# Second layer: latent queries and one gate block with 512 moving columns over two weight places

## The chip, the cores and the metric

One core of a Trainium2 chip runs the whole forward pass. The metric is the device time of one execution in microseconds (us). The kernel before was timed three times; the median is 1577.26 us (1575.3 to 1577.57).

## What is computed

A backbone of two layers over 1024 latent tokens and 256 context tokens, all with 1024 features. Layer 1 is windowed attention with 16 heads. Layer 2 is latent attention, which the change concerns:

```
hx = rms_norm(x) * (1 + scale) + shift               # 1024 latent tokens; hc likewise, 256 context tokens
cq, ckv, kr, g = split(h @ w_in, [512, 256, 32, 1024])
q  = (rms_norm(cq, q_norm) @ w_uq)                   # 16 heads of 64 (nope) + 32 (rope)
kv = (rms_norm(ckv, kv_norm) @ w_ukv)                # 16 heads of 64 (keys) + 64 (values)
o  = softmax(q k^T) v                                # latent queries, context and latent keys
x  = x + gate * ((o * silu(g)) @ w_out)
```

A final RMSNorm gives the output. All inputs are float32. Of the second layer the change touches the product that gives `cq` (the latent queries, 512 columns) and a quarter of the product that gives `g` (the gates, 1024 columns).

## The kernel before, in words

Every product is split for precision: both operands are kept as a high and a low part, and `mm3` (L126 to L130) issues three matmuls for each block of 128 contracted features: high times high (L128), low times high (L129), high times low (L130). A matmul takes a stationary operand of 128 columns, loaded ahead of it, and streams the moving operand's columns; a PSUM bank of the kernel (`PB`) holds 512 of them.

The second layer's input is kept transposed in SBUF, in pairs of two token tiles: `hT1[p]` holds 256 tokens, pair 0 the context and pairs 1 to 4 the latent tokens. Each is 16 KB of a partition, in rows of 256 elements: eight rows (one for each 128 features) of the high part, then eight of the low part. The places, in KB of an arena: pair 0 at 134, pair 1 at 80, pair 2 at 0, pair 3 at 16, pair 4 at 32 (L981). The weights are loaded in ten blocks by `fetch1` (L1007): DMAs on SP into a ring of three stage buffers, then a split in two, the high part by ACT (L123), the low part by POOL or DVE (L124). A weight block of 256 columns has the same layout of 16 KB, and its place is given by `wst1` (L982): 96, 48, 96, 96, 48, 96, 64, 48, 96, 48. Blocks 1 and 2 are the two halves of the latent queries' weights (48 and 96), block 3 the rope queries' (96), blocks 4 and 5 the other queries' (48 and 96), blocks 6 to 9 the gates' (block 7 at 48, block 8 at 96, block 9 at 48).

The stages follow one another on TensorE (PE) in this order:

- keys and values (`kv_tile`) with gate block 6 between, from about 720 to 783 us;
- eight latent-query tiles (`cq_tile`, L1072), one for each 128 tokens: the tokens are the stationary operand, the weights the moving one, first the 256 columns of block 1, then those of block 2, eight rows and three matmuls each, 48 matmuls into the halves of one PSUM bank. Behind each: the sum of squares (ACT L1014), the root (POOL L1016), the scaling (DVE L1085); two tiles later four transposes (PE L1090) and a split by ACT and DVE into `cqT`, the transposed queries (high part at 64 to 80 KB of the same arena, low part in another arena);
- eight rope-query tiles (`qr_tile`, L1096), then sixteen tiles of the other queries (`qn_tile`), all with 512 moving columns, 12 matmuls each;
- gate block 7 for pairs 1 to 4 (`g_tile`, L1135, called at L1195): here the weights are stationary and a pair's 256 tokens the moving operand, 48 matmuls for each pair; ACT applies Silu to the 128x512 result (L1152) and SP stores it (L1154). Beside it the value and key weights are loaded and split (the value weights go to 64 to 80 KB, where the queries' high part was);
- block 9 is fetched behind block 7 into the same place (L1197); gate blocks 8 and 9 follow, partly within the attention;
- the attention, from about 949 us, in an order of PE, ACT and DVE that is written out by hand, and the output product between and behind.

Ahead of the attention the order of each engine's work is set by the Tile scheduler when the kernel is built, by program order as priority and by its own estimate of times. Waits between engines are set from what each instruction reads and writes.

Of the kernel before, what the change touches and what calls it, by code (L numbers as in the profile page):

```python
# [12 lines left out]
AF = mybir.ActivationFunctionType  # L13
# [10 lines left out]
NP = TOK // 256  # L24
EPS = 1e-6
KB = 256
# [21 lines left out]
def shp(ap, *dims):  # L48
    n = 1
    for d in dims:  # L50
        n *= d
    ap = ap[:, 0:n]
    if len(dims) == 1:
        return ap
    names = "abcdefg"[: len(dims)]
    kw = {c: d for c, d in zip(names[1:], dims[1:])}
    return ap.rearrange("p (" + " ".join(names) + ") -> p " + " ".join(names), **kw)
# [3 lines left out]
def kernel(ctx: ExitStack, tc: tile.TileContext, t, out, dbg=None):  # L61
    nc = tc.nc
# [5 lines left out]
    R = cpool.tile([128, int(R_KB * KB)], F32R, name="arena_r")  # L68
# [10 lines left out]
    g1_d = dpool.tile([8, 128, SEQ], F32, name="g1_d")  # L79
# [3 lines left out]
    load = nc.sync.dma_start  # L83
    load2 = nc.scalar.dma_start

    def r_at(kb, *dims):
        n = int(np.prod(dims))
        if kb >= 114:
            return shp(R2[:, int((kb - 114) * KB) : int((kb - 114) * KB) + n], *dims)
        return shp(R[:, int(kb * KB) : int(kb * KB) + n], *dims)  # L90
# [27 lines left out]
    pss = Banks(0, 1, 2, 3, 4, 5)  # L118
    pst = Banks(6, 7)

    def split(hi, lo, src, lo_eng=None):

        nc.scalar.copy(hi, src)  # L123
        (lo_eng or nc.vector).tensor_sub(lo, src, hi.bitcast(F32))  # L124

    def mm3(o, a, b, first, last):  # L126
        (ah, al), (bh, bl) = a, b
        nc.tensor.matmul(o, ah, bh, start=first, stop=False)  # L128
        nc.tensor.matmul(o, al, bh, start=False, stop=False)  # L129
        nc.tensor.matmul(o, ah, bl, start=False, stop=last)  # L130
# [174 lines left out]
    ev = Ring(F, [38, 40, 42, 44], 512)  # L305
# [17 lines left out]
    class Pieces:  # L323
# [6 lines left out]
        def load(self, n=1):  # L330
            for _ in range(n):
                if self.todo:
                    bi, k = self.todo.pop(0)
                    c0 = blocks[bi]
                    st = shp(stg.next(), 2, 256)
                    src = w_in[k * 128 : (k + 2) * 128, c0 : c0 + 256]
                    load(out=st, in_=src.rearrange("(k p) n -> p k n", p=128))
                    self.held.append((bi, k, st))
# [139 lines left out]
    def proj_t(bi, gp, c):  # L478

        W = wt[bi]  # L480
        ps = pss()
        if gp:
            o = shp(ps, 2, 256)
            m = [hw[gp][:, :, s] for s in range(2)]
        else:
            o = ps[:, 0:258]
            m = [hT[0][:, s] for s in range(2)]
        cs = slice(c * 128, c * 128 + 128)
        for k in range(8):
            b = [x[:, :, k, :] if gp else x[:, k, :] for x in m]  # L490
            mm3(o, [W[:, s, k, cs] for s in range(2)], b, k == 0, k == 7)
        if gp == 0:
            bias[bi, c] = biases()
            nc.scalar.copy(bias[bi, c], ps[:, 256:258])
        return ps
# [264 lines left out]
    class RawRing:  # L760
        i = 5
# [108 lines left out]
    for c in range(2):  # L870
        ps = proj_t(1, 0, c)
# [14 lines left out]
    for bi in (8, 9):  # L886
        for c in range(2):
            ps = proj_t(bi, 0, c)
# [40 lines left out]
    for ui, u in enumerate(units):  # L929
# [11 lines left out]
        for ci in range(u.m):  # L941
# [10 lines left out]
            i = u.g * u.m + ci - 1  # L952
# [28 lines left out]
    hT1 = [r_at(o, 2, 8, 256) for o in (134, 80, 0, 16, 32)]  # L981
# [11 lines left out]
    ev = Ring(F, [2, 4, 6, 12], 512)  # L993
# [8 lines left out]
    blocks1 = [("kv", 512, 288), ("cq", 0, 256), ("cq", 256, 256)]  # L1002
    blocks1 += [("qr", 1024, 512), ("qn", 0, 512), ("qn", 512, 512)]
    blocks1 += [("g", 800 + c * 256, 256) for c in range(4)]
    wt1 = {}

    def fetch1(bi, eng=None):  # L1007
        kind, c0, n = blocks1[bi]
        nk = 4 if kind[0] == "q" else 8
        wt1[bi] = r_at(wst1[bi], 2, nk, n)  # L1010
        load_w(wt1[bi], t["b_w_uq"] if kind[0] == "q" else w_in1, stg, nk, n, lo_eng=eng, col0=c0)

    def rstd(ps, n, st):
        nc.scalar.activation(junk[:, 0:n], ps, AF.Square, accum_out=st[:, 0:1])  # L1014
        nc.vector.tensor_scalar(st[:, 1:2], st[:, 0:1], 1.0 / n, EPS, ALU.mult, ALU.add)
        nc.gpsimd.tensor_tensor(st[:, 2:3], st[:, 1:2], mhalf, ALU.pow)  # L1016
        return st[:, 2:3]
# [22 lines left out]
    def kv_tile(ti):  # L1040
# [28 lines left out]

        pend.append(rest)  # L1070

    def cq_tile(ti):  # L1072
        p, j = (ti + 2) // 2, ti % 2
        ps = pss()
        for c in range(2):
            for k in range(8):
                mm3(
                    ps[:, c * 256 : c * 256 + 256],
                    [hT1[p][:, s, k, j * 128 : j * 128 + 128] for s in range(2)],
                    [wt1[1 + c][:, s, k, :] for s in range(2)],  # L1080
                    k == 0, k == 7,
                )
        r = rstd(ps, 512, sm_ring())
        e = ev.next()
        nc.vector.scalar_tensor_tensor(e, ps, r, qn, ALU.mult, ALU.mult)  # L1085

        def rest():
            pt = shp(pst(), 4, 128)
            for c in range(4):
                nc.tensor.transpose(pt[:, c, :], e[:, c * 128 : c * 128 + 128], ident)  # L1090
            ts = slice(ti * 128, ti * 128 + 128)
            split(cqT[0][:, :, ts], cqT[1][:, :, ts], pt)

        pend.append(rest)
# [40 lines left out]
    def g_tile(bi, p, half=None, bank=None):  # L1135
        c0 = blocks1[bi][1]
        W = wt1[bi]
        if half != 1:
            gps[bi] = pss() if bank is None else bank
        ps = gps[bi]  # L1140
        for j in (0, 1) if half is None else (half,):
            for k in range(8):
                mm3(
                    ps[:, j * 256 : j * 256 + 256],
                    [W[:, s, k, j * 128 : j * 128 + 128] for s in range(2)],
                    [hT1[p][:, s, k, :] for s in range(2)],
                    k == 0, k == 7,
                )
        if half == 0:
            return  # L1150
        gg = ev.next()
        nc.scalar.activation(gg, ps, AF.Silu)  # L1152
        ch = (c0 - 800) // 128
        load(out=g1_d[ch : ch + 2, :, (p - 1) * 256 : p * 256].rearrange("c p n -> p c n"), in_=shp(gg, 2, 256))  # L1154

    nx = norm_x(src1(4), xr, junk)
    for ti in range(NT):
        n = ti + 3
# [13 lines left out]
    for ti in range(8):  # L1172
        cq_tile(ti)
        flush(2)
# [13 lines left out]
    for k in range(2):  # L1188
        for c in range(4):
# [2 lines left out]
            dst = ukK if c < 2 else ukV  # L1192
            cs = slice((c % 2) * 512, (c % 2) * 512 + 512)
            split(dst[:, 0, k, cs], dst[:, 1, k, cs], st, nc.gpsimd)
    for p in range(1, NP):  # L1195
        g_tile(7, p)
    fetch1(9)  # L1197


# [532 lines left out]
```

## Time and profile before

| | |
|---|---|
| median of three runs | 1577.26 us |
| the profiled execution, device time | 1574.73 us |
| its span, first to last instruction | 1573.0 us |
| PE busy | 1538.7 us (98%), 9846 matmuls |
| PE's weight loads busy | 1228.6 us (78%) |
| VectorE (DVE), ScalarE (ACT), GpSimd (POOL) busy | 993.5, 772.8, 753.8 us |
| mean granted TensorE clock | 0.995 |

The profile shows one execution. Engines run side by side, so busy times do not add up to the span. "PE" are the matmuls, "PEld" their weight loads, which overlap the matmuls; SPq is the queue from which SP issues DMAs. Matmuls are pipelined: each lasts longer than the distance to the next one's start, and it is the distance that adds up. Rows of the order of time show the start, the duration, the engine, the line, the operation, what it writes and reads, the shape, a count where equal neighbours are merged, and in brackets the idle time ahead of it with what ended it.

### The profile page before, as it was taken

The page shows a single profiled execution, that of the slowest core. Times are in us where ns is not written, and L with a number is a line of the kernel's source. Part 1 is how long each engine was busy: PE and PEld are TensorE (multiplying, and loading weights), DVE is VectorE, ACT ScalarE, POOL GpSimd, SP SyncE. Part 2 cuts the span into 40 slices and gives each one's busy share as a digit, 9 for nine tenths or more (in the row PEclk, how much of TensorE's full clock was granted, in tenths as well). Part 3 has the DMA queues.
Part 4 walks back from the last instruction along what each step waited for, and adds up shares of the span by engine and source line. Part 5 has one row for each costly group of instructions (what it writes and reads, how often), then busy time and mean ns, then how long its engine had stood idle before and what let it go on. Part 6 is the DMA issues. An engine that isn't in the chain of part 4 may idle for free.

```text
span 1573.0 us, 26868 instructions
## 1 busy us (share of the span) xinstructions
PE 1538.7 (98%) x9846; PEld 1228.6 (78%) x9846; DVE 993.5 (63%) x1757; ACT 772.8 (49%) x1492; POOL 753.8 (48%) x810
## 2 busy tenths in 40 slices
PE   7999999999999999998999999999999999999998
PEld 4988888887878888888998899666766766766687
DVE  3878996657777777768425203666567566567354
ACT  4432322267777777767313323455555555555322
POOL 1151211136564444544105140588688688689410
PEclk9999999999999999999999999999999999999999
DMA  8357774653343222345105753313233233244251
GB/s 316 114 159 219 199 207 137 200 164 99 99 146 100 85 89 85 95 132 182 48 1 156 262 151 98 91 45 98 61 98 101 71 91 88 61 138 113 69 168 68
DMA packets 148277, 192.83 MB, mean 123 GB/s; under 512 B 13985, under 2 KB 86177, under 8 KB 148145
## 3 DMA queue, kind: packets, MB, share of 16 engines
q1 hardware_dynamic: 146672, 188.94, 40.2%
q10 hardware_dynamic: 1472, 2.16, 0.5%
q8 instruction: 78, 1.28, 0.3%
q14 instruction: 55, 0.44, 0.1%
HBM read 144.90 MB, written 46.15 MB: 121 GB/s over the span
## 4 chain that ended last, share of the span: by engine, by line
PE 81%; DVE 8%; issue 3%; DMA 3%; ACT 2%; POOL 2%; SPq 0%; DVEq 0%; POOLq 0%; ACTq 0%
PE PB L128 12%; PE PB L129 12%; PE PB L130 12%; PE PB L1359 12%; PE PB L1381 9%; PE PB L621 5%; PE PB L662 5%; PE PB L1322 4%; PE PB L652 4%; DVE arena_f L193 2%; DVE arena_f L519 1%; DMA arena_f<-a_w_in 1%; PE PB L1330 1%; PE PB L1410 1%; ACT arena_r L123 1%
## 5 line engine op out<-in xcount | busy, mean ns | idle before, releaser
L128 PE MATMUL PB<-arena_r 128*128 128x512 f32 (+3 forms) x1216 | 410.8, 339 | 5.5 <-ACT arena_r L423 2.4
L129 PE MATMUL PB<-arena_r 128*128 128x512 f32 (+3 forms) x1184 | 395.2, 334 | 1.8 <-POOL arena_r L689 0.8
L130 PE MATMUL PB<-arena_r 128*128 128x256 f32 (+3 forms) x1152 | 381.5, 332 | 0.2 <-DVE arena_r L124 0.2
L1373 POOL TENSOR_TENSOR arena_f<-arena_f 128x512 f32<-128x512 f32 x252 | 324.9, 1289 | 79.7 <-ACT arena_f L1365 62.9
L128 PEld LDWEIGHTS PB<-arena_r 128*128 128x128 f32 x1216 | 231.1, 191 | 32.2 <-ACT arena_r L423 4.8
L129 PEld LDWEIGHTS PB<-arena_r 128*128 128x128 f32 x1184 | 226.4, 191 | 22.9 <-DVE arena_r L424 2.4
L124 POOL TENSOR_TENSOR arena_r<-arena_f,arena_r 128x512 fp32r<-128x512 f32 x80 | 109.3, 1381 | 276.8 <-ACT arena_r L123 226.8
L130 PEld LDWEIGHTS PB<-arena_r 128*128 128x128 f32 x1152 | 220.4, 191 | 20.7 <-issue 1.7
L1365 ACT ACTIVATE arena_f<-PB 128x1024 f32<-128x1024 f32 x160 | 164.1, 1027 | 108.5 <-PE PB L1359 68.4
L1324 DVE TENSOR_REDUCE arena_f<-PB 128x1 f32<-128x1024 f32 x128 | 156.0, 1219 | 86.7 <-PE PB L1322 86.6
L1359 PE MATMUL PB<-arena_r 64*128 64x512 f32 (+1 forms) x1500 | 195.1, 392 | 0.3 <-ACT arena_f L1365 0.3
L1359 PEld LDWEIGHTS PB<-arena_r 64*128 64x128 f32 (+1 forms) x1500 | 137.1, 185 | 28.9 <-ACT arena_f L1365 1.8
L124 DVE TENSOR_TENSOR arena_r<-PB,arena_r 128x512 fp32r<-128x512 f32 x168 | 114.6, 689 | 61.1 <-ACT arena_r L123 60.2
L1381 PE MATMUL PB<-arena_f 128*64 128x512 f32 x640 | 144.4, 597 | 0.0
L632 DVE CUSTOM_DVE_ANT_0 arena_f<-PB,arena_f,small 128x640 f32<-128x640 f32 (+2 forms) x176 | 125.2, 722 | 19.5 <-PE PB L621 11.6
L635 ACT ACTIVATE arena_f<-arena_f,small 128x640 f32<-128x640 f32 (+2 forms) x160 | 119.5, 747 | 35.1 <-DVE small L632 32.6
L123 ACT CAST arena_r<-PB 128x512 fp32r<-128x512 f32 x176 | 101.7, 585 | 46.6 <-PE PB L652 44.6
L621 PE MATMUL PB<-arena_k,arena_r 128*128 128x256 f32 (+1 forms) x576 | 111.2, 308 | 1.5 <-DVE small L632 1.3
L1381 PEld LDWEIGHTS PB<-arena_f 128*64 128x64 f32 x640 | 43.1, 136 | 83.2 <-issue 79.9
L652 PE MATMUL PB<-ident,arena_f 128*128 128x128 f32 x672 | 104.0, 274 | 0.6 <-DVE arena_r L124 0.3
L123 ACT CAST arena_r<-arena_f 128x512 fp32r<-128x512 f32 (+2 forms) x121 | 72.0, 605 | 62.1 <-DMA arena_f<-a_w_in 14.5
L621 PEld LDWEIGHTS PB<-arena_k,arena_r 128*128 128x128 f32 x576 | 89.2, 189 | 13.9 <-DVE small L632 3.5
(213 smaller groups left out, 2532.5 us busy)
## 6 DMA issues: line engine op xcount, KB each, us to landing
arena_f<-ada_w SPq DMA_DIRECT2D x40, 512.0 KB, 4.8
arena_r<-q_d SPq DMA_DIRECT2D x80, 256.0 KB, 4.1
arena_r<-qn_d SPq DMA_DIRECT2D x64, 256.0 KB, 4.0
arena_r<-qr_d SPq DMA_DIRECT2D x172, 64.0 KB, 3.4
arena_f<-a_w_in SPq DMA_DIRECT2D x40, 256.0 KB, 3.1
g_d<-arena_f SPq DMA_DIRECT2D x32, 256.0 KB, 2.6
q_d<-arena_f SPq DMA_DIRECT2D x64, 128.0 KB, 2.5
qn_d<-arena_f SPq DMA_DIRECT2D x16, 512.0 KB, 5.3
```

The costliest lines, as they stand in the source:

```text
L123: nc.scalar.copy(hi, src)
L124: (lo_eng or nc.vector).tensor_sub(lo, src, hi.bitcast(F32))
L128: nc.tensor.matmul(o, ah, bh, start=first, stop=False)
L129: nc.tensor.matmul(o, al, bh, start=False, stop=False)
L130: nc.tensor.matmul(o, ah, bl, start=False, stop=last)
L621: nc.tensor.matmul(S[:, at : at + n], qT[:, s, hq, :], kT[:, g, k : k + n], start=s == 0, stop=s == 1)
L652: nc.tensor.transpose(pt[:, h, :], self.Ps[h][:, ci * 128 : ci * 128 + 128], ident)
L1324: nc.vector.reduce_max(mx[:, 32 + b : 33 + b], flat, AX.X, negate=True)
L1359: nc.tensor.matmul(S[:, t], k[r, c : c + 128], q[r], start=j == 0, stop=j == 4)
L1365: nc.scalar.activation(E, self.S, AF.Exp)
L1373: eng.tensor_add(self.acc, self.acc, E[:, t])
L1381: nc.tensor.matmul(self.pv[p : p + 64], Vq[:, cs[t], self.h % 4, :], E[:, t], start=i == 0, stop=i == 4)
```

## The change

In `cq_tile`, tile 0 stays. For tiles 1 to 7 the two halves of the weights, blocks 1 and 2, are read as one moving operand of 512 columns: two runs of 256 that lie 48 KB apart, taken by a view (`stride48`) of the arena. Each row of features then has three matmuls of 512 columns and not six of 256.

For gate block 7, `g_tile` over pairs 1 to 4 is replaced by `g_pair` over two token pairs at a time: pairs 2 and 3 (16 KB apart, view `stride16`), then pairs 4 and 1 (32 and 80 KB, so 48 KB apart). A weight of 128 columns is stationary for 512 tokens; each half j of the block gets a PSUM bank of its own, one Silu over 512 columns, and two stores, one for each pair of tokens.

```diff
+    stride48 = R[:, 18 * KB : 114 * KB].rearrange("p (c k n) -> p c k n", c=2, n=256)
+    stride16 = R[:, 0 : 32 * KB].rearrange("p (c k n) -> p c k n", c=2, n=256)
+
+    def g_pair(bi, ps, view, k0):
+        W = wt1[bi]
+        ch = (blocks1[bi][1] - 800) // 128
+        for j in range(2):
+            o = shp(pss(), 2, 256)
+            for k in range(8):
+                mm3(
+                    o,
+                    [W[:, s, k, j * 128 : j * 128 + 128] for s in range(2)],
+                    [view[:, :, k0 + 8 * s + k, :] for s in range(2)],
+                    k == 0, k == 7,
+                )
+            gg = shp(ev.next(), 2, 256)
+            nc.scalar.activation(gg, o, AF.Silu)
+            for i, p in enumerate(ps):
+                load(out=g1_d[ch + j, :, (p - 1) * 256 : p * 256], in_=gg[:, i])
+
     def cq_tile(ti):
         p, j = (ti + 2) // 2, ti % 2
         ps = pss()
-        for c in range(2):
+        for c in range(2 if ti == 0 else 1):
             for k in range(8):
-                mm3(
-                    ps[:, c * 256 : c * 256 + 256],
-                    [hT1[p][:, s, k, j * 128 : j * 128 + 128] for s in range(2)],
-                    [wt1[1 + c][:, s, k, :] for s in range(2)],
-                    k == 0, k == 7,
-                )
+                h = [hT1[p][:, s, k, j * 128 : j * 128 + 128] for s in range(2)]
+                if ti:
+                    mm3(shp(ps, 2, 256), h, [stride48[:, :, 30 + 8 * s + k, :] for s in range(2)], k == 0, k == 7)
+                else:
+                    mm3(
+                        ps[:, c * 256 : c * 256 + 256], h,
+                        [wt1[1 + c][:, s, k, :] for s in range(2)],
+                        k == 0, k == 7,
+                    )
...
-    for p in range(1, NP):
-        g_tile(7, p)
+    g_pair(7, (2, 3), stride16, 0)
+    g_pair(7, (4, 1), stride48, 14)
     fetch1(9)
```

## The prediction

> **What bounds the kernel now.** I read the page first (busy shares and the chain that ended last), then PE's waits in the stretch that the change touches, then the stretches, then the order of the products there.
>
> ```profile
> span 1573.0 us, 26868 instructions
> ...
> PE 1538.7 (98%) x9846; PEld 1228.6 (78%) x9846; DVE 993.5 (63%) x1757; ACT 772.8 (49%) x1492; POOL 753.8 (48%) x810
> ...
> PE 81%; DVE 8%; issue 3%; DMA 3%; ACT 2%; POOL 2%; SPq 0%; DVEq 0%; POOLq 0%; ACTq 0%
> ```
>
> PE is busy 98% of the span and carries 81% of the last chain. That is an average; the two places of the change are read for themselves. PE's waits from 760 to 970 us are a list of one row:
>
> ```profile
> PE PB L130 <- DVE arena_r L124: 0.2, 1, 0.2
> ```
>
> And the busy times of a query tile (first row), of the first half of gate block 7 (second row) and of the attention behind (third row):
>
> ```profile
> core 0: us, PE busy (x) PEld busy (x) DVE busy (x) ACT busy (x) POOL busy (x), PEclk, DMA share, GB/s
> ...
> 794.60:800.40 5.80, 5.80 (x51) 5.80 (x50) 1.24 (x3) 0.95 (x3) 0.55 (x1) 1.00 0.01 3
> ...
> 902.80:914.00 11.20, 11.20 (x95) 11.20 (x94) 1.00 (x3) 4.08 (x8) 7.84 (x7) 1.00 0.84 256
> ...
> 949.00:1560.00 611.00, 607.55 (x4177) 421.78 (x4175) 372.36 (x492) 289.44 (x400) 399.88 (x322) 1.00 0.32 90
> ```
>
> In both places PE and its weight loads have no gap, at granted clock 1.00, and from 949 us on PE stands still for 3.5 us of 611. So time taken from the products at 789 to 926 us moves everything behind them forward, unless something there hangs on a transfer or on another engine.
>
> **What a product costs.** A matmul's own duration is of no use here (they overlap); the distance from one start to the next is. One query tile of 48 products with 256 columns, between two groups of four transposes (L1090):
>
> ```profile
> 800.46 0.60 PE L1090 MATMUL PB<-ident,arena_f 128*128 128x128 f32 x4
> 800.82 0.36 PE L128 MATMUL PB<-arena_r 128*128 128x256 f32 x1
> 801.02 0.28 PE L129 MATMUL PB<-arena_r 128*128 128x256 f32 x1
> ...
> 806.54 0.28 PE L130 MATMUL PB<-arena_r 128*128 128x256 f32 x1
> 806.66 0.60 PE L1090 MATMUL PB<-ident,arena_f 128*128 128x128 f32 x4
> ```
>
> The tile takes 806.66 - 800.46 = 6.20 us: 0.36 for the transposes, 0.20 to the second product, then 46 distances of (806.54 - 801.02)/46 = 0.120 and a last one to the transposes. Block 7 is 192 such products without transposes between:
>
> ```profile
> 902.79 0.28 PE L128 MATMUL PB<-arena_r 128*128 128x256 f32 x1
> ...
> 925.82 0.28 PE L128 MATMUL PB<-arena_r 128*128 128x256 f32 x1
> ```
>
> The second row is the first product of block 8, so block 7 takes 23.03 us, again 0.120 each. Products with 512 columns stand just ahead of it, 168 of them (14 tiles of 12), behind a group of transposes:
>
> ```profile
> 864.58 0.48 PE L128 MATMUL PB<-arena_r 128*128 128x512 f32 x1
> 864.89 0.40 PE L129 MATMUL PB<-arena_r 128*128 128x512 f32 x1
> ...
> 866.98 0.39 PE L129 MATMUL PB<-arena_r 128*128 128x512 f32 x1
> ...
> 902.56 0.39 PE L130 MATMUL PB<-arena_k,arena_r 128*128 128x512 f32 x1
> ```
>
> The first distance is 0.31; the next nine are (866.98 - 864.89)/9 = 0.232; the other 157 are (902.56 - 866.98)/157 = 0.2266. So one product of 512 columns replaces two of 256 at 0.2266 for 0.240: 13 ns saved, 8 ns in the first ten behind transposes. The arithmetic is the same; only a fixed part of some 13 ns per product goes.
>
> The Trainium skill, page "TensorE: Matmul & The Clock Gate", section "Back-to-back issue gap", speaks against the change: it gives the warm distance as N/2.4 ns plus only 2.5 ns. By that a pair would save 2.5 ns, and all 264 removed products 0.7 us, an estimate from the page. The trace does not agree (0.120 and 0.2266 are N/2.4 plus 13), and the sum goes by the trace.
>
> **The change, part by part.**
>
> *Query tiles.* Tile 0 stays; tiles 1 to 7 have 24 products of 512 columns for 48 of 256 (168 fewer). New tile: 0.36 for the transposes, 0.31, nine of 0.232 (2.09), thirteen of 0.2266 (2.95), 0.23 to the next transposes: 5.94 us, which is 0.26 less. Seven tiles: **1.8 us**. If the slower 0.232 lasts the whole run, a tile takes 0.36 + 0.31 + 22 x 0.232 + 0.23 = 6.00 and seven save 1.4; if 0.2266 holds from the second distance on, 5.89 and 2.2. Both weight blocks must now be in place at the start of tile 1. They are: tile 0 reads all of both first, as now, and waits for nothing.
>
> *Two places.* The moving operand comes as two runs of 256 columns, 48 KB apart in a partition (16 KB in the first half of block 7). Layer 1 has that form already (two places 16 KB apart):
>
> ```profile
> 299.72 0.39 PE L129 MATMUL PB<-arena_r 128*128 128x512 f32 x1
> ...
> 304.93 0.39 PE L128 MATMUL PB<-arena_r 128*128 128x512 f32 x1
> ```
>
> That is 23 distances of 0.2265, the same as from one place. I cost the second place at nothing; 48 KB is not in the trace.
>
> *Gate block 7.* 96 products of 512 columns for 192 of 256: 96 x 0.2266 = 21.75 for 23.03, **1.28 us**. Nothing but the like products stands ahead, so the start-up distances do not come back; at 0.232 throughout it would be 0.8.
>
> *Its stores.* Four Silu evictions of 128x512 stay four. Four stores become eight of half the size, on SP, whose queue also issues the loads of the last weight block (9):
>
> ```profile
> 910.90 0.38 SPq L1154 DMA_DIRECT2D g_d<-arena_f  x1
> 919.99 0.38 SPq L279 DMA_DIRECT2D arena_f<-b_w_in  x1
> 920.42 0.46 SPq L1154 DMA_DIRECT2D g_d<-arena_f  x1
> ...
> 927.56 0.37 SPq L279 DMA_DIRECT2D arena_f<-b_w_in  x1
> ```
>
> Four more issues of 0.46 are 1.8 us of SP. Who waits behind them is block 9's first product:
>
> ```profile
> 922.35 1.30 POOL L124 TENSOR_TENSOR arena_r<-arena_f,arena_r 128x512 fp32r<-128x512 f32 x1 [1.13 <-ACT arena_r L123]
> ...
> 931.06 1.29 POOL L124 TENSOR_TENSOR arena_r<-arena_f,arena_r 128x512 fp32r<-128x512 f32 x1 [1.02 <-ACT arena_r L123]
> ```
> ```profile
> 937.34 0.28 PE L128 MATMUL PB<-arena_r 128*128 128x256 f32 x1
> ```
>
> Its last piece is ready at 931.06 + 1.29 = 932.35 and the block begins at 937.34 now. Begun 3.4 us earlier, with the pieces 1.8 later and not themselves earlier, 934.15 would face 933.94, where only the first piece is needed at once and the last 18 products (2.2 us) later. So nothing is lost; without that cover it would be 1.8 us.
>
> *The first rope-query tile.* Its weights take the place of query block 2 row by row, as the last query tile lets go of them, and the fourth piece is late:
>
> ```profile
> 829.35 2.06 ACT L123 CAST arena_r<-arena_f 128x512 fp32r<-128x512 f32 x3 [2.69 <-PE PB L129]
> ...
> 834.49 0.68 DVE L124 TENSOR_TENSOR arena_r<-arena_f,arena_r 128x512 fp32r<-128x512 f32 x1
> ```
> ```profile
> 831.43 0.60 PE L1090 MATMUL PB<-ident,arena_f 128*128 128x128 f32 x4
> ...
> 834.63 0.38 PE L1090 MATMUL PB<-ident,arena_f 128*128 128x128 f32 x2
> 835.23 0.50 PE L130 MATMUL PB<-arena_r 128*128 128x512 f32 x1 [0.21 <-DVE arena_r L124]
> ...
> 838.54 0.60 PE L1090 MATMUL PB<-ident,arena_f 128*128 128x128 f32 x4
> 841.73 0.60 PE L1109 MATMUL PB<-ident,arena_f 128*128 128x128 f32 x4
> ```
>
> Two tiles take 838.54 - 831.43 = 7.11 us there, where the next takes 3.19, so 0.7 are lost: a wait of 0.21 and a transpose group cut in two. Now the last tile reads block 2 only in its second half (2.9 us); then over the whole 5.4 us, in the order of the rows. The first three pieces are free earlier, the stage buffer of the first piece with them, so the fourth load starts sooner; its rows still come free at the very end. Bounds: 0.7 gained if the tile runs like the next, 0.2 lost if the split falls once more behind tile 7's own DVE work. I take **0.3**. The next block (4) takes the other place, which is now read to the end of the tile; it is needed 30 us later.
>
> *The sum.* 1.8 + 1.28 + 0.3 = 3.4 us. The profiled execution took 1574.73 us around its span of 1573.0, and becomes 1571.3. The median of the runs shown, 1577.26, is 2.5 above it; against it the same 3.4 give **1573.9 us**, or 0.21% less. About 0.2% (3.15 us) is what a measurement of this kernel can tell from no change, so the forecast stands on that line.
>
> **The rivals.**
>
> 1. *The long products stay at the slow pace and the late piece stays late.* For it: the rope-query tile of 12 from 838.54 to 841.73 leaves (3.19 - 0.36 - 0.31)/11 = 0.229 for a distance, so each tile starts slow anew. Against it: 12 are too few to reach 0.2266, which the 168 products do after ten. 1.4 + 0.8 + 0 = 2.2 us: 1575.1.
>
> 2. *Nothing is gained.* Either 512 columns from places 48 KB apart cost what two halves cost (0.240), or a wait behind takes the gain. For it: 48 KB is not in the trace. Against it: 16 KB shows nothing, and the one PE wait up to 970 us is the 0.21. 1577.3. The page's 2.5 ns would end close by, at 1576.6.
>
> 3. *Slower: the two-place view counts as one span of memory when the waits are set.* The query tiles' view then covers 64 to 80 KB, where the transposed queries are written, and the second half of block 7 covers the same place, where the value weights are written till 922.35 + 1.30 = 923.65. Each of the tiles 3 to 7 would wait for the cast of the transposes just ahead:
>
> ```profile
> 801.31 0.58 ACT L123 CAST arena_r<-PB 128x512 fp32r<-128x512 f32 x1
> ```
>
> From 800.82 to 801.89 is 1.07 us, five times 5.4; block 7's second half would stand ready near 911.6 (902.79 + 10.9 - 2.1) and start near 921.5, 9.9 us. Less the 3.4: up to 11.9 slower, 1589; the tiles alone, once they wait, already outweigh the gain (1579.3). Against it: rope-query tile 2 reads rows of the low halves between which the last query tile's low half is written, in program order ahead of it, and does not wait:
>
> ```profile
> 839.90 0.40 PE L129 MATMUL PB<-arena_r,arena_k 128*128 128x512 f32 x1
> ...
> 840.62 0.69 DVE L124 TENSOR_TENSOR arena_k<-PB,arena_r 128x512 fp32r<-128x512 f32 x1 [0.53 <-ACT arena_r L123]
> ```
>
> Taken as one span, the write to 841.31 would have held the read at 839.90.
>
> **How the numbers follow.** The forecast with its bounds (2.8 to 4.2 us gained) has 0.62, rival 1 0.2, rival 2 0.1, rival 3 0.08. The range reaches from the best case (2.2 + 1.28 + 0.7 = 4.2) against the lowest run shown, 1575.3, to no gain against the median: 1571.1 to 1577.3. That leaves out rival 3 and some spread. More than 3.15 us faster: seven tenths of the forecast and a little of rival 1, 0.46. Within 0.2%: the rest of both and rival 2, 0.46. Slower: 0.08.
>
> **What would show it.** The span from 789 to 926 us shorter by 3.4; 264 fewer products; tiles at 5.94 us between transposes; block 7 at 21.75; no new row among PE's waits before 970 us; the first two rope-query tiles in under 7 us; the attention unchanged in length. Wrong, if the distances of 512 columns in the tiles are 0.24, if PE waits for ACT or POOL in a query tile or in the middle of block 7, or if block 9 waits for its weights.

## The result and the profile after

The changed kernel took 1572.7 us in the median of six runs (1571.56 to 1574.62), the kernel before 1577.41 in six, three of them the runs given above. The ratio is 0.9968, with a 95% interval of 0.9956 to 0.9979. A second timing, later and with more runs, gave 0.9975 (0.9965 to 0.9985). Both intervals lie below 1, so it is faster. The traces say more closely by how much: 3.8 us, a ratio of 0.9976, which lies in both intervals. That rests on one execution of the kernel before and two of the changed one, which agree to 0.03 us in the stretch compared below.

The page of the changed kernel, busy times and the chain that ended last:

```profile
span 1569.1 us, 26349 instructions
...
PE 1535.1 (98%) x9582; PEld 1213.5 (77%) x9582; DVE 1005.9 (64%) x1757; ACT 772.1 (49%) x1492; POOL 751.0 (48%) x810
...
PE 85%; DVE 5%; issue 3%; POOL 3%; ACT 2%; DMA 2%; SPq 0%; POOLq 0%; DVEq 0%; ACTq 0%
```

There are 264 fewer matmuls (9582 for 9846), and PE is still the bound. The span is 3.9 us shorter, but a span also holds what happens ahead of the change, and that differs between executions of one program. So I measure one stretch throughout: from the last product of the key tiles (288 columns), with everything ahead of it unchanged, to the first transposes of the keys' rope part, where the order written by hand begins. The two rows of the kernel before, then of the changed one:

```profile
776.65 0.30 PE L130 MATMUL PB<-arena_r 128*128 128x288 f32 x1
...
948.86 1.03 PE L1229 MATMUL PB<-ident,krF 128*32 128x128 f32 x8
```
```profile
776.45 0.29 PE L130 MATMUL PB<-arena_r 128*128 128x288 f32 x1
...
944.86 1.03 PE L1252 MATMUL PB<-ident,krF 128*32 128x128 f32 x8
```

172.21 us before, 168.41 after: 3.80 less. Behind the stretch nothing changed: 1573.0 - 948.86 = 624.1 us before, 1569.1 - 944.86 = 624.2 after. Ahead of it 0.2 us went another way by chance.

Inside the stretch, in order of time. A query tile of the changed kernel (L1113 are its transposes):

```profile
805.62 0.60 PE L1113 MATMUL PB<-ident,arena_f 128*128 128x128 f32 x4
805.98 0.49 PE L128 MATMUL PB<-arena_r 128*128 128x512 f32 x1
...
811.56 0.60 PE L1113 MATMUL PB<-ident,arena_f 128*128 128x128 f32 x4
```

5.94 us for 6.20. Then the two first rope-query tiles, again by the transposes ahead of each and behind the second:

```profile
829.36 0.60 PE L1113 MATMUL PB<-ident,arena_f 128*128 128x128 f32 x4
...
832.58 0.60 PE L1113 MATMUL PB<-ident,arena_f 128*128 128x128 f32 x4
...
835.79 0.60 PE L1113 MATMUL PB<-ident,arena_f 128*128 128x128 f32 x4
```

6.43 us for 7.11; the wait and the divided group are gone. Then block 7, from its first product to the first of block 8:

```profile
900.07 0.39 PE L128 MATMUL PB<-arena_r 128*128 128x512 f32 x1
...
921.83 0.28 PE L128 MATMUL PB<-arena_r 128*128 128x256 f32 x1
```

21.76 us for 23.03. Against the kernel before, the transposes at 829.36 stand 2.07 earlier (831.43), those at 835.79 2.75 earlier (838.54), block 8's first product 3.99 earlier (925.82). Less the 0.2 from ahead: 1.87 from the tiles, 0.68 at the rope-query tiles, 1.24 from block 7 and the products in between, and nothing is given back behind it. PE's waits from 742 to 970 us are an empty list.

### The profile page after: what moved, and what is told of

Read it like the earlier page. It is cut to its first block, busy times and chain, and to the rows that moved or that the text cites. A ratio compares the mean times of both kernels' runs of the same rounds, so it can differ in the third digit from the quotient of the medians.

```text
span 1569.1 us, 26349 instructions
## 1 busy us (share of the span) xinstructions
PE 1535.1 (98%) x9582; PEld 1213.5 (77%) x9582; DVE 1005.9 (64%) x1757; ACT 772.1 (49%) x1492; POOL 751.0 (48%) x810
## 4 chain that ended last, share of the span: by engine, by line
PE 85%; DVE 5%; issue 3%; POOL 3%; ACT 2%; DMA 2%; SPq 0%; POOLq 0%; DVEq 0%; ACTq 0%
PE PB L128 14%; PE PB L129 14%; PE PB L130 14%; PE PB L1382 12%; PE PB L1404 9%; PE PB L621 4%; PE PB L1345 4%; PE PB L662 4%; PE PB L652 4%; PE PB L1353 1%; DVE arena_f L193 1%; PE PB L1433 1%; ACT arena_r L123 1%; PE PB L681 1%; PE PB L412 1%
## 5 line engine op out<-in xcount | busy, mean ns | idle before, releaser
L128 PE MATMUL PB<-arena_r 128*128 128x512 f32 (+3 forms) x1128 | 394.8, 352 | 5.5 <-ACT arena_r L423 2.4
L129 PE MATMUL PB<-arena_r 128*128 128x512 f32 (+3 forms) x1096 | 378.9, 346 | 1.8 <-POOL arena_r L689 0.8
L1396 POOL TENSOR_TENSOR arena_f<-arena_f 128x512 f32<-128x512 f32 x252 | 328.3, 1303 | 82.3 <-ACT arena_f L1388 65.4
L130 PE MATMUL PB<-arena_r 128*128 128x512 f32 (+3 forms) x1064 | 365.5, 344 | 0.0
L128 PEld LDWEIGHTS PB<-arena_r 128*128 128x128 f32 x1128 | 213.6, 190 | 35.2 <-ACT arena_r L423 4.8
L129 PEld LDWEIGHTS PB<-arena_r 128*128 128x128 f32 x1096 | 208.9, 191 | 26.1 <-DVE arena_r L424 2.4
L130 PEld LDWEIGHTS PB<-arena_r 128*128 128x128 f32 x1064 | 202.7, 191 | 24.0 <-issue 1.7
```

Source lines behind the costliest of these rows:

```text
L1396: eng.tensor_add(self.acc, self.acc, E[:, t])
```

## The experiments

**Each part alone.** In the first run the call of block 7 is put back; in the second the query tiles are.

```diff
-    g_pair(7, (2, 3), stride16, 0)
-    g_pair(7, (4, 1), stride48, 14)
+    for p in range(1, NP):
+        g_tile(7, p)
```
```diff
-        for c in range(2 if ti == 0 else 1):
+        for c in range(2):
...
-                if ti:
+                if False:
```

> Only the latent-query tiles 1 to 7 are changed; gate block 7 is as before. Theory (each part gives its own saving, PE carries it to the end): a tile takes 5.94 us between transposes for 6.20, the first transposes of the rope-query tiles end the seven tiles 1.8 us earlier, the rope-query tiles lose another 0.7, so the span is 2.5 us below 1573.0; block 7 stays at 23.03 us. Rival (the saving of a part is swallowed at the next late weight block when the other part is missing): less than 1.5 us of the span.

> Only gate block 7 is changed; the query tiles are as before. Theory: block 7 takes 21.75 us for 23.03, the rope-query tiles keep their wait of 0.2 us and their 7.11 us for two, so the span is 1.3 us below 1573.0. Rival (the eight stores or the last weight block eat the gain): a wait of PE ahead of block 9 and less than 0.6 us of the span.

The stretch with the query tiles alone, then with block 7 alone:

```profile
778.60 0.29 PE L130 MATMUL PB<-arena_r 128*128 128x288 f32 x1
...
948.28 1.03 PE L1252 MATMUL PB<-ident,krF 128*32 128x128 f32 x8
```
```profile
776.14 0.29 PE L130 MATMUL PB<-arena_r 128*128 128x288 f32 x1
...
947.09 1.03 PE L1252 MATMUL PB<-ident,krF 128*32 128x128 f32 x8
```

169.68 and 170.95 us: 2.53 and 1.26 less than before, and their sum is 3.79, the whole. The expectations named the spans; these came out as 1572.2 and 1571.0, so that the smaller part seems to gain more: 0.8 us with the tiles, which taken alone would speak for the rival, and 2.0 with block 7. That is the part ahead: the stretch begins at 778.60 in one and at 776.14 in the other. In the run with block 7 alone PE keeps its wait of 0.2 us at the first rope-query tile. The times follow the stretches: 0.9982 (0.9973 to 0.9991) with the tiles, 0.9991 (0.9980 to 1.0002) with block 7, which alone cannot be told from no change. By the stretches neither part swallows the other's gain.

**Why the fourth piece of the rope-query weights came in time.** One run widens the last query tile alone, the other tiles 1 to 6 alone; block 7 is as before in both.

```diff
-        for c in range(2 if ti == 0 else 1):
+        for c in range(1 if ti == 7 else 2):
...
-                if ti:
+                if ti == 7:
```
```diff
-        for c in range(2 if ti == 0 else 1):
+        for c in range(1 if 0 < ti < 7 else 2):
...
-                if ti:
+                if 0 < ti < 7:
```

> Of the query tiles only the last, 7, has the 512 columns; tiles 1 to 6 and block 7 are as before. Theory (the late fourth piece of the rope-query weights came from the order in which the last tile lets go of the rows of block 2): tile 7 saves 0.26 us and the two rope-query tiles 0.7 us, together 0.95; no wait at the first of them. Rival (the scheduler's order of the instructions differs because the tiles before are shorter): only 0.26 us, and the wait of 0.2 us and the divided group of transposes stay.

> Query tiles 1 to 6 have the 512 columns; the last tile, 7, and block 7 are as before. Theory (order of release in the last tile): the six tiles save 6 x 0.26 = 1.6 us, the two rope-query tiles take 7.1 us as before, with the wait. Rival (order of the scheduler, or the shift as such): 1.6 + 0.7 = 2.3 us and no wait.

The transposes about the first two rope-query tiles, first with the last tile widened, then with the six others:

```profile
833.92 0.60 PE L1113 MATMUL PB<-ident,arena_f 128*128 128x128 f32 x4
...
840.34 0.60 PE L1113 MATMUL PB<-ident,arena_f 128*128 128x128 f32 x4
```
```profile
831.62 0.60 PE L1113 MATMUL PB<-ident,arena_f 128*128 128x128 f32 x4
...
834.94 0.38 PE L1113 MATMUL PB<-ident,arena_f 128*128 128x128 f32 x2
...
838.72 0.60 PE L1113 MATMUL PB<-ident,arena_f 128*128 128x128 f32 x4
```

6.42 us with the last tile alone, 7.10 and the divided group with the six others. The stretches agree:

```profile
779.42 0.29 PE L130 MATMUL PB<-arena_r 128*128 128x288 f32 x1
...
950.69 1.03 PE L1252 MATMUL PB<-ident,krF 128*32 128x128 f32 x8
```
```profile
778.46 0.29 PE L130 MATMUL PB<-arena_r 128*128 128x288 f32 x1
...
949.07 1.03 PE L1252 MATMUL PB<-ident,krF 128*32 128x128 f32 x8
```

171.27 and 170.61: 0.94 and 1.60 less, as the theory had it to 0.01. So the last tile is worth 0.94 and the six others together 1.60: the 0.68 comes with the last tile's own order of rows, and neither the shift nor the shorter tiles ahead bring it. The changed kernel shows the chain, in rows of DVE, SP and ACT; the row of SP in the kernel before stands below them:

```profile
826.49 1.47 DVE L124 TENSOR_TENSOR arena_r<-arena_f,arena_r 128x512 fp32r<-128x512 f32 x2
827.20 4.37 SPq L279 DMA_DIRECT2D arena_f<-b_w_uq  x4
...
829.87 0.62 ACT L123 CAST arena_r<-arena_f 128x512 fp32r<-128x512 f32 x1 [1.28 <-DMA arena_f<-b_w_uq]
...
830.52 0.69 DVE L124 TENSOR_TENSOR arena_r<-arena_f,arena_r 128x512 fp32r<-128x512 f32 x1 [1.20 <-ACT arena_r L123]
```
```profile
830.72 11.19 SPq L279 DMA_DIRECT2D arena_f<-b_w_uq  x8
```

The first low part is done while the last tile still runs, its stage buffer is free, the fourth load starts at 827.20 (830.72 before, in the kernel whose last tile ended 2 us later), and its low part is ready at 831.21, ahead of tile 7's own work on DVE (835.17 before, behind it). With the last tile alone the low part also stands ahead of that work, with the six others behind it. The earlier load and the earlier place on DVE thus came together, and no run separates what each is worth.

**What the 13 ns are.** The kernel before, with block 7 in products of 128 columns:

```diff
+                for n in (0, 128):
+                    ...
+                        ps[:, j * 256 + n : j * 256 + n + 128],
+                        [W[:, s, k, j * 128 : j * 128 + 128] for s in range(2)],
+                        [hT1[p][:, s, k, n : n + 128] for s in range(2)],
```

> The kernel before, but block 7 in 384 products of 128 columns for 192 of 256: the same columns, twice the weight loads. Theory (a product costs its columns and a fixed part): the distances 0.120 and 0.2266 us lie on a line of 0.416 ns per column and 13 ns fixed, so 128 columns take 0.067 and the block 25.6 us for 23.03. Rival (the distance of 256 columns is that of the weight loads, whose engine row shows no gap there, and only by chance near the line): 128 columns take 0.120 again and the block 46 us.

First product of block 7, first product of block 8:

```profile
906.29 0.22 PE L128 MATMUL PB<-arena_r 128*128 128x128 f32 x1
...
949.12 0.34 PE L128 MATMUL PB<-arena_r 128*128 128x256 f32 x1
```

42.83 us for 384 products: 0.1115 each. Both expectations miss: 0.067 is far off, and 0.120 is not it either. Twice the weight loads in the same columns nearly double the block, and a product of half the columns saves 8 ns only. So something other than the columns holds a product of 128 columns to 0.1115, and at 256 columns a product (0.120) stands just above that. The line of columns plus 13 ns holds from 256 to 512 and does not go on to 128. That the weight load is what holds it is the likely reading, not shown: no run has two narrow products share one load. PE's and its loads' busy time in 13 us of block 7, with 128, 256 (the kernel before) and 512 columns (the changed kernel):

```profile
907.00:920.00 13.00, 13.00 (x111) 13.00 (x110) 0.00 (x0) 5.43 (x9) 8.84 (x8) 1.00 0.69 197
```
```profile
907.00:920.00 13.00, 13.00 (x119) 13.00 (x118) 1.00 (x3) 3.18 (x6) 7.88 (x7) 1.00 0.68 205
```
```profile
907.00:920.00 13.00, 13.00 (x59) 10.76 (x58) 0.00 (x0) 5.34 (x9) 8.80 (x8) 1.00 0.70 197
```

The loads have no gap at 128 and 256 columns. At 512 they stand idle for 2.24 us of 13, and the 13 ns a product are there all the same; what these 13 ns are stays open. The Trainium skill, page "TensorE: Matmul & The Clock Gate", section "LDWEIGHTS (loading the stationary operand)", gives a load's time in ns as its columns divided by 1.2, so 107 ns for 128 columns, an estimate from the page. The distance of 0.1115 us agrees with that to 5 ns; the loads' own records last 0.19 us in this run and overlap, so they do not show it.

**Further than the change.** Five kernels widen more: the query tile that was left, tile 0; with it block 8 for pairs 1 and 2, 80 KB apart; two attempts at blocks 6, 8 and 9 together; and at the end block 6 alone. The first two:

```diff
-        for c in range(2 if ti == 0 else 1):
+        for c in range(1):
...
-                if ti:
+                if True:
```
```diff
-    for p in range(1, 3):
-        g_tile(8, p)
+    g_pair2(8, 1, 2)
...
+        row = v[:, 0:256]
+        return (x, y), lambda r: bass.AP(
+            row.tensor, v[:, r * 256 : r * 256 + 256].offset, [tuple(row.ap[0]), (gap, 2), (1, 256)]
+        )
```

> The changed kernel with query tile 0 at 512 columns too, nothing else. Theory: 0.26 us less, without a wait, as the low part of block 2's last piece was ready at 782.9 us of the trace before, when tile 0 began at 782.7. Rival: tile 0 waits for it, and the gain is gone.

> The changed kernel with query tile 0 at 512 columns, and block 8 for pairs 1 and 2 as products of 512 columns from two places 80 KB apart. Theory (the second place costs nothing at any distance): 0.2266 us a product, 48 x 13 ns = 0.6 us less than with tile 0 alone. Rival (far places are slow): 0.24 us or more a product, and no gain. The gates of block 8 for pairs 1 and 2 are the one thing that is read in another way; what comes of them is not what is asked here.

The stretch with tile 0, and with tile 0 and block 8:

```profile
775.60 0.29 PE L130 MATMUL PB<-arena_r 128*128 128x288 f32 x1
...
943.73 1.03 PE L1252 MATMUL PB<-ident,krF 128*32 128x128 f32 x8
```
```profile
776.57 0.29 PE L130 MATMUL PB<-arena_r 128*128 128x288 f32 x1
...
944.05 1.03 PE L1279 MATMUL PB<-ident,krF 128*32 128x128 f32 x8
```

168.13 and 167.48: 0.28 below the changed kernel, and another 0.65 for block 8. Both theories hold, and places 80 KB apart cost nothing either; each of the two is one execution. Timed beside the changed kernel and the kernel before:

> The changed kernel with query tile 0 at 512 columns too, for its time: 4.1 us below the kernel before (3.8 and 0.28 from the traces), a ratio of 0.9974. If times move with more than the trace shows, the ratio is nearer to 0.9968, that of the changed kernel, or below.

> The changed kernel once more, beside the same runs of the kernel before: 3.8 us less by the trace, a ratio of 0.9976. The first timing said 0.9968 with 0.9956 to 0.9979; if the trace holds all of the gain, this one comes out nearer to 0.9976.

0.9971 (0.9961 to 0.9981) with tile 0 and 0.9975 (0.9965 to 0.9985) for the changed kernel again. The traces' 0.9974 and 0.9976 lie in them; the two cannot be told apart by their times.

The two larger attempts:

```diff
-        if ti > 1 and ti % 2:
+        if ti in (3, 5):
             g_tile(6, ti // 2)
+        if ti == 9:
+            g_pair2(6, 3, 4)
...
-    for p in range(1, 3):
-        g_tile(8, p)
-    g_tile(9, 1)
+    g_pair2(8, 1, 2)
+    g_pair2(9, 1, 2)
     units[0].prep()
     units[1].prep()
-    g_tile(9, 2)
```

> The changed kernel, and on top of it block 6 for pairs 3 and 4, and blocks 8 and 9 for pairs 1 and 2 (80 KB apart), as products of 512 columns. Theory (13 ns for each product removed, wherever PE has no gap): 48 + 96 products fewer, 0.6 + 1.3 = 1.9 us below the changed kernel, from the first change to the attention. Rival (the fillers are missed: gate block 6 of pair 3 filled waits of the key tiles, and the first attention loads start 6 us later, behind block 9): a wait in the key tiles or at the start of the attention, and under 1 us in all.

> As the run with more blocks widened, and query tile 0 with 512 columns too. Theory: another 0.26 us, so 2.2 us below the changed kernel and 6.0 below the kernel before, a ratio of 0.996. Rival (block 2 of the weights is not split when tile 0 wants both blocks at its start): a wait of PE of over 0.3 us in tile 0, and nothing gained by it.

In these two the scaled latents of key tiles 8 and 9 are overwritten by those of query tiles 0 and 1 before they are transposed, so the keys and values of 256 tokens are other numbers; the instructions are the same in kind and count. The timed one came out at 0.9974 (0.9966 to 0.9983) where 0.996 was expected, no better than the changed kernel. PE's waits from 780 to 950 us in it (the other, with a profile alone, has the same row):

```profile
PE PB L1066 <- DVE arena_f L1135: 0.8, 2, 0.4
```

The transposes of the last two key tiles (L1066) wait for the scaling of query tiles (L1135), 0.4 us each. That is neither of the two mechanisms in the expectations. Both results of block 6 for pairs 3 and 4 now stand behind key tile 9, so the ring of four result buffers comes round before these transposes are issued: they read buffers that query tiles 0 and 1 have written in between. From the first product of key tile 6 to the transposes of the keys' rope part the two kernels take 186.91 and 186.57 us, the changed one 187.54 (rows below): 0.6 and 1.0 less, where 1.9 and 2.2 were expected. The last run keeps the fillers' places, one half behind key tile 7 and one behind 9:

```diff
+        if ti in (7, 9):
+            g_pair(6, (3, 4), R[:, 16 * KB : 48 * KB].rearrange("p (c k n) -> p c k n", c=2, n=256), 0, [(ti - 7) // 2])
```

> The changed kernel, with tile 0 at 512 columns, and block 6 of pairs 3 and 4 as two products of 512 columns that stay where the two of 256 stood, one behind key tile 7 and one behind key tile 9, so that a filler remains between the key tiles. Theory (13 ns for each product removed where PE has no gap; what the run with more blocks lost was the missing filler): 0.28 for tile 0 and 48 x 13 ns = 0.6, so 0.9 us below the changed kernel, 4.7 below the kernel before, and no new wait of PE in the key tiles. Rival (the key tiles lose with any shift of block 6): the transposes of the keys wait again, 0.4 us at a time, and the gain is 0.3 or less.

PE has no wait from 742 to 950 us in it, so the rival falls. Its time, 0.9977 (0.9966 to 0.9987), shows neither the gain of 0.9 us nor its absence. Half of block 6 lies ahead of the stretch used so far, but a longer one, from the first product of key tile 6, holds all of it. The rows of the changed kernel, of the run with tile 0 alone and of this one:

```profile
757.32 0.38 PE L128 MATMUL PB<-arena_r 128*128 128x288 f32 x1
...
944.86 1.03 PE L1252 MATMUL PB<-ident,krF 128*32 128x128 f32 x8
```
```profile
756.48 0.38 PE L128 MATMUL PB<-arena_r 128*128 128x288 f32 x1
...
943.73 1.03 PE L1252 MATMUL PB<-ident,krF 128*32 128x128 f32 x8
```
```profile
760.76 0.38 PE L128 MATMUL PB<-arena_r 128*128 128x288 f32 x1
...
947.38 1.03 PE L1254 MATMUL PB<-ident,krF 128*32 128x128 f32 x8
```

187.54, 187.25 and 186.62 us: block 6 saves 0.63 and both together 0.92, as the theory had it. That is one execution of this kernel. A version with blocks 6, 8 and 9 widened and the fillers in their places was not run.

## Why the prediction was right

*Query tiles.* 1.8 us was taken, 5.94 a tile; 1.87 and 5.93 to 5.94 were measured. The slow first ten distances behind each group of transposes were rightly counted: the rival that they last the whole tile (6.00) and the bound that they don't occur (5.89) are both out.

*Two places.* The second place cost nothing, at 16, 48 and 80 KB.

*Gate block 7.* 21.75 predicted, 21.76 measured. The eight stores and block 9's weights held nothing up.

*The first rope-query tile.* This is the term that was mis-sized: 0.3 was taken between bounds of -0.2 and 0.7, and 0.68 came. The mechanism stood in the working in full (rows let go in order, an earlier stage buffer, an earlier fourth load), but I halved it for fear that the split would fall behind tile 7's own DVE work once more. In the changed kernel it stands ahead of that work.

*The sum.* 3.4 us against 3.8 in the trace; the missing 0.4 is that term. Against the median 1573.9 was given and 1572.7 measured. Of the first timing's 0.32%, about 5 us, the traces show 3.8; the rest is within its interval, and the second timing does not have it. The chances were even between faster and within 0.2%, and the trace's 0.24% is only just on the faster side of that line. That it came out on this side is in part luck: the extra 0.4 us of the rope-query tiles was not in the forecast.

*The rivals.* Rival 1 fell with the tiles' 5.94, rival 2 with block 7. Rival 3, the view taken as one span of memory, would have put PE's waits into the tiles and into the middle of block 7; there is none. The argument against it, a row of the rope-query tiles in the kernel before, carried over. The Trainium skill's 2.5 ns per product (page "TensorE: Matmul & The Clock Gate", section "Back-to-back issue gap"), which that section gives for the isolated gap of a product and not for a stream with weight loads, do not hold here: they would have given 0.7 us for the 264 products, an estimate from the page, and the tiles and block 7 gave 3.1.

## What to carry to other kernels

Where PE has no gap, the price of a product is the distance between starts, at the width used and at the width planned, read from the same trace: here 0.120 and 0.2266 us, so that doubling the width saves 13 ns a pair and no more. In one tile the gain of the wider products can be smaller than what they do to the release of their operands: here the last tile's row order gave 0.68 us, as much as two and a half tiles' products. And a part ahead of the change that differs by several microseconds between executions hides such gains in the span; measure between two landmarks that frame the change.

## What was not expected of the hardware

A product of 128 columns takes 0.1115 us where one of 256 takes 0.120: going from 256 columns down to 128 gains next to nothing for products of this kind.

The same program started its last key product at 776.45 us in one execution and at 780.55 in another, with spans of 1569.1 and 1573.3, while the stretch behind took 168.41 and 168.38:

```profile
780.55 0.29 PE L130 MATMUL PB<-arena_r 128*128 128x288 f32 x1
...
948.93 1.03 PE L1252 MATMUL PB<-ident,krF 128*32 128x128 f32 x8
```

The difference of these two thus comes from ahead of the change. Most of it arises about 240 us. Busy times from 239 to 243 us, the shorter execution first (the number behind POOL's is the granted clock):

```profile
239.00:243.00 4.00, 4.00 (x22) 3.41 (x22) 3.44 (x7) 0.00 (x0) 0.00 (x0) 1.00 0.84 277
```
```profile
239.00:243.00 4.00, 4.00 (x14) 3.42 (x14) 3.18 (x7) 0.00 (x0) 0.00 (x0) 0.51 0.80 280
```

At a granted clock of 0.51 PE starts 14 products there in place of 22. Product by product, the second execution is 0.6 us ahead of the first at 220 us and 3.2 behind at 260. Why the clock was lower in one of them stays open.
